# Splitting the shared value weights into the place of memT, in a two-layer decoder trunk

## The chip, the cores and the metric

The kernel runs on one core of a Trainium2 chip. The metric is the device time of one execution in microseconds (us); lower is better. Times of several runs are given as their median. The profile is of one execution, which has a time of its own; its span runs from the first instruction to the last.

## The reference

The input is one sequence of 256 positions of width 2048, a memory of 256 tokens of the same width, and fp32 weights. There are two layers. Each multiplies the residual stream by one input matrix whose columns are a main-branch input (1536), its gate (1536), memory queries (512) and their gate (512).

```python
for i in range(DEPTH):
    if i == N_A_LAYERS:
        k_blocks, v_blocks, k_mean = moba_shared_kv(h, w_kv_shared)
    u = h @ w_in[i]
    branch_in, gate_b, mem_q, gate_m = jnp.split(u, split_at, axis=-1)
    if i < N_A_LAYERS:
        branch = multiscale_pool(branch_in, pool_w[i], pool_scale[i])
    else:
        branch = moba_attention(branch_in, k_blocks, v_blocks, k_mean)
    mem_o = memory_attention(mem_q, mem, w_mem_kv[i])
    mixed = jnp.concatenate([branch * silu(gate_b), mem_o * silu(gate_m)], axis=-1)
    h = layer_norm(DEEPNORM_ALPHA * h + mixed @ w_out[i], ln_g[i], ln_b[i])
```

In the first layer the main branch is a pooling over trailing windows. In the second it is causal attention with 12 heads of 128. Its keys and values come from the shared weights `w_kv_shared`: the "shared keys" are the first 1536 columns, the "shared values" the last 1536. With 256 positions there is one attention block, so the block selection chooses nothing. In both layers there is also a 4-head attention into the memory, with keys and values `mem @ w_mem_kv[i]`.

## The kernel before

**Precision.** Every fp32 operand of TensorE is split into a high part (a copy into the type fp32r, by ScalarE, line 70) and a low part (value minus high part, by VectorE, line 71). A product is then three products: high by high, high by low and low by high.

**Items.** All weights come in blocks of 128 x 1024 fp32, 512 KB. Each block is an item in one long list, written out in the order in which TensorE uses the blocks. `run` walks the list: at step i it splits item i+3, issues the load of item i+4 on SP's queue, emits the matmuls of item i, and then whatever small steps were put down for that point (`later`). The order on each engine is therefore the order in which the program writes the instructions; no scheduler moves them. Loads land in a rotating set of four buffers `raw`; high and low parts stand in rotating sets of four buffers `wh` and `wl` each. A buffer is written again when its last readers are done. An item may name another destination: kind "act" for activations, and kind "keep" with a pair of places for the two parts; `prep_piece` then writes there and draws no `wh` and `wl`.

**Two forms of product.** `proj_t` (line 155) has the weight block stationary and the transposed activations moving: per 128 x 128 of weights one matmul of 512 columns (high weights by [high | low] activations) and one of 256 (low weights by high activations). `proj_n` (line 181) has the activations stationary and the weights moving: per block 12 matmuls of 512 columns, in triples high by high, high by low, low by high. Each accumulates in PSUM tiles `acc`.

**Tiles.** One large tile `xm` holds the transposed stream `xT` in its first half and the transposed memory `memT` in its second, each 16 blocks of 512 columns, both as views that begin SHIFT = 40 elements later than the half. At the end of the kernel the same two halves hold `kept`, views without the shift: the high and low parts of the last quarter of the second output projection, which are split ahead into it. `zT` holds the gated branches for the output projections.

```python
xm = sb.tile([P, 2 * KT * 2 * T + 128], F32R, name="xm")
KX = KT * 2 * T
xT, memT = (xm[:, SHIFT + i * KX:SHIFT + (i + 1) * KX].rearrange("p (k t) -> p k t", k=KT) for i in range(2))
kept = [xm[:, i * KX:(i + 1) * KX].rearrange("p (k n) -> p k n", k=KT) for i in range(2)]
```

**Order of the work.** First layer: memory keys and values, memory queries and gate, the pooling branch, output projection (`out_0`). Then memory keys and values of the second layer (`mem_k(1)`, `mem_v(1)`), during which the stream is normalised and transposed into `xT`; these are the last readers of `memT`. Then memory queries and gate, and three groups of four heads. A group is 8 blocks of shared keys, 8 of queries, 8 of gate (all `proj_t`), and 8 of shared values (`proj_n`, stationary `xT`). The attention steps of a group are woven in between. Last comes `out_1`, the second output projection: three quarters by items, with the kept blocks of the fourth quarter between them, then the fourth quarter from `kept` (`last`, line 715), in a closing part with the final normalisation.

Of the kernel before, what the change touches and what calls it, by code (L numbers as in the profile page):

```python
# [32 lines left out]
BLK = 1024  # L33
# [11 lines left out]
def trunk(ctx: ExitStack, tc: tile.TileContext, a: dict, out: bass.AP):  # L45
# [10 lines left out]
    xT, memT = (xm[:, SHIFT + i * KX:SHIFT + (i + 1) * KX].rearrange("p (k t) -> p k t", k=KT) for i in range(2))  # L56
# [8 lines left out]
    def mm(o, l, r, start, stop):  # L65
        nc.tensor.matmul(o, l, r, start=start, stop=stop)  # L66

    def split(hi, lo, src):

        nc.scalar.activation(hi, src, AF.Copy)  # L70
        nc.vector.tensor_sub(lo, src, f(hi))  # L71
# [12 lines left out]
    def item(src, cols, consume=None, dst=None):  # L84
        items.append(dict(src=src, cols=cols, consume=consume, dst=dst, cuts=(0, cols)))
# [69 lines left out]
    def proj_t(mov, wblk, done):  # L155


        acc = []

        def consume(kb):  # L160
            def go(wh, wl, k0=0, k1=4):
                if not acc:
                    acc.extend(ps.tile([P, 512], F32, name="acc", bufs=4) for _ in range(2))
                h = wh.rearrange("p (k n) -> p k n", n=256)
                l = wl.rearrange("p (k n) -> p k n", n=256)
                for n in range(2):
                    s = slice(n * P, (n + 1) * P)
                    for kk in range(k0, k1):
                        k = 4 * kb + kk
                        if k < KT - 1:  # L170
                            mm(acc[n], h[:, kk, s], mov[:, k], k == 0, False)
                        mm(acc[n][:, :T], l[:, kk, s], mov[:, k, :T], False, False)
                        if k == KT - 1:
                            mm(acc[n], h[:, kk, s], mov[:, k], False, True)
                    if kb == 3:
                        done(n, acc[n])
            return go
        for kb in range(4):
            item(wblk[kb], BLK, consume(kb))

    def proj_n(sta, wblk, done, korder=range(8), banks=("acc", "acc")):

        acc = []
        korder = list(korder)

        def consume(j, kb):
            def go(wh, wl):
                if j == 0:
                    acc.extend(ps.tile([P, 512], F32, name=b, bufs=4 if b == "acc" else 1) for b in banks)
                h = wh.rearrange("p (k n) -> p k n", n=512)  # L190
                l = wl.rearrange("p (k n) -> p k n", n=512)
                for t in range(2):
                    for kk in range(2):
                        k = 2 * kb + kk
                        xh = sta[:, k, t * P:(t + 1) * P]
                        xl = sta[:, k, T + t * P:T + (t + 1) * P]
                        first, last = j == 0 and kk == 0, j == 7 and kk == 1
                        mm(acc[t], xh, h[:, kk], first, False)
                        mm(acc[t], xh, l[:, kk], False, False)
                        mm(acc[t], xl, h[:, kk], False, last)  # L200
                    if j == 7:
                        done(t, acc[t])
            return go
        for j, kb in enumerate(korder):
            item(wblk[kb], BLK, consume(j, kb))

    def fold(dst, acc):
        nc.scalar.activation(dst, acc[:, T:], AF.Copy)  # L208
# [2 lines left out]
    def to_heads(dst, base):  # L211
        def done(n, acc):
            s = sb.tile([P, T], F32, name="fold", bufs=3)
            hi, lo = dst()[:, base + n, :T], dst()[:, base + n, T:]
            fold(s, acc)
            nc.vector.tensor_copy(hi, s)
            nc.vector.tensor_sub(lo, s, f(hi))
        return done

    def to_gate(dst, base):  # L220

        def done(n, acc):
            s = sb.tile([P, T], F32, name="fold", bufs=3)
            fold(s, acc)
            g = dst()

            def finish():
                th = sb.tile([P, T], F32, name="th", bufs=2)
                nc.scalar.activation(th, s, AF.Tanh, scale=0.5)
                nc.vector.scalar_tensor_tensor(g[:, base + n, :], th, 1.0, s,  # L230
                                               op0=ALU.add, op1=ALU.mult)
            later(1, finish)
        return done

    def to_values(dst):
        def done(t, acc):
            split(dst()[:, t, 0], dst()[:, t, 1], acc)
        return done

    def heads_tile(name):  # L240
        return sb.tile([P, 4, 2 * T], F32R, name=name)
# [126 lines left out]
    def plan(pr, a, b, c):  # L368

        later(a, pr.a)  # L370
        later(a + 1, pr.exps)
        later(a + 2, pr.divide)
        later(b, lambda: pr.b(0))
        later(b + 1, lambda: pr.b(1))
        later(c, pr.c)
# [68 lines left out]
    def fresh(key, make):  # L444

        tiles = []

        def g():
            if not tiles:
                tiles.append(make())  # L450
                st[key] = tiles[0]
            return tiles[0]
        return g
# [12 lines left out]
    def mem_v(layer, banks=("acc", "acc")):  # L466
        v = fresh("v", val_tile)
        proj_n(memT, [a["w_mv"][layer, kb] for kb in range(8)], to_values(v), banks=banks)

    def w_in(layer, c):  # L470
        return [a["w_in"][layer, c, kb] for kb in range(4)]

    def after(fn):

        it = items[-1]
        old = it["consume"]

        def go(*w):
            if old is not None:
                old(*w)  # L480
            fn()
        it["consume"] = go

    def mem_q_gate(layer):
        q = fresh("q", lambda: heads_tile("qq"))
        g = fresh("g", gate_tile)
        for c in range(2):
            proj_t(xT, w_in(layer, 12 + c), to_heads(q, 2 * c))
        prs = [MemPair(0, st), MemPair(2, st)]

        def go():
            plan(prs[0], 1, 5, 9)
            plan(prs[1], 7, 11, 14)
        after(go)
        for c in range(2):
            proj_t(xT, w_in(layer, 14 + c), to_gate(g, 2 * c))
# [94 lines left out]
    def out_0(n):  # L591
        proj_n(zT, [a["w_out"][0, n, kb] for kb in range(8)], to_residual(n), KORDER)
# [42 lines left out]
    mem_v(1)  # L635


    mem_q_gate(1)
    for grp in range(3):
        k = fresh("k", lambda: heads_tile("kk"))  # L640
        q = fresh("q", lambda: heads_tile("qq"))
        g = fresh("g", gate_tile)
        v = fresh("v", val_tile)
        for c in range(2):
            proj_t(xT, [a["w_sk"][2 * grp + c, kb] for kb in range(4)], to_heads(k, 2 * c))
        for c in range(2):
            proj_t(xT, w_in(1, 2 * grp + c), to_heads(q, 2 * c))
        prs = [MobaPair(2 * j, 4 * grp + 2 * j, st) for j in range(2)]

        def go(prs=prs):  # L650
            plan(prs[0], 1, 5, 17)
            plan(prs[1], 7, 18, 20)
        after(go)
        for c in range(2):
            proj_t(xT, w_in(1, 6 + 2 * grp + c), to_gate(g, 2 * c))
        proj_n(xT, [a["w_sv"][grp, kb] for kb in range(8)], to_values(v))


    def out_1():
# [25 lines left out]
    for j, it in enumerate(collect(out_1)):  # L685
# [3 lines left out]
        if j >= 8 and j % 2:  # L689
            kb = (j - 8) // 2  # L690
# [155 lines left out]
```

## Time and profile before

| | |
|---|---|
| median of 3 runs | 825.08 us (825.01 to 825.12) |
| profiled execution: its time | 824.92 us |
| its span, first to last instruction | 823.0 us |
| TensorE matmul busy | 810.0 us, 98% of the span |
| VectorE busy | 558.7 us, 68% |
| ScalarE busy | 397.1 us, 48% |
| granted TensorE clock, mean | 0.996 |

PE is TensorE's matmuls, PEld its weight loads, DVE is VectorE, ACT is ScalarE, POOL is GpSimd and SP the engine that issues most loads. L66 is line 66, the helper through which every matmul goes, so its rows are told apart by their tiles: `acc<-wh,xm` is a matmul into `acc` that reads `wh` and `xm`. A matmul's shown length reaches to its modelled end, after the next one has begun; how fast matmuls follow each other is read from their starts, or from a stretch's length over their count. An idle time in square brackets is what the engine sat idle before the instruction, with what ended it.

### The profile page before, as it was taken

The numbers are of one execution on the slowest core, as the hardware profiler recorded it, in microseconds if no ns is written. First come the engines' busy times: TensorE is split into PE (matmuls) and PEld (weight loads), VectorE is DVE, ScalarE is ACT, GpSimd is POOL, SyncE is SP. The second block draws the span as 40 slices with busy tenths as digits, with TensorE's granted clock in tenths as the row PEclk, the third lists the DMA queues.
The fourth block names the chain that finished last, engine by engine and source line by source line (L and its number), as shares of the span: only waits on it lengthen the run. The fifth ranks groups of instructions, "written<-read, shape, count | busy, mean of one in ns | idle before, by whom it ended". The sixth has DMA issues, their size and how long they took to land.

```text
span 823.0 us, 11533 instructions
## 1 busy us (share of the span) xinstructions
PE 810.0 (98%) x4436; PEld 700.7 (85%) x4436; DVE 558.7 (68%) x793; ACT 397.1 (48%) x578; POOL 0.2 (0%) x4
## 2 busy tenths in 40 slices
PE   7999999999999999999999999999999999999996
PEld 6888888898888888888888888888888888888885
DVE  5786668657956555797667667575765667568746
ACT  6564545545545343544455445344554445545520
POOL 0000000000000000000000000000000000000000
PEclk9999999999999999999999999999999999999998
DMA  8975445456557655675554544645454554646842
GB/s 311 302 251 204 173 154 191 171 181 216 179 192 283 212 191 193 203 235 201 181 179 144 189 160 173 201 156 192 169 172 169 186 188 156 185 151 224 285 130 102
DMA packets 47163, 159.13 MB, mean 193 GB/s; under 512 B 5375, under 2 KB 7167, under 8 KB 46847
## 3 DMA queue, kind: packets, MB, share of 16 engines
q1 hardware_dynamic: 46080, 155.47, 55.8%
q10 hardware_dynamic: 1028, 2.93, 0.9%
q8 instruction: 34, 0.56, 0.3%
q14 instruction: 21, 0.17, 0.1%
HBM read 156.28 MB, written 2.10 MB: 192 GB/s over the span
## 4 chain that ended last, share of the span: by engine, by line
PE 98%; DVE 1%; DMA 1%; SPq 0%; ACT 0%; issue 0%; DVEq 0%
PE acc L66 89%; PE o L66 4%; PE s L66 2%; PE pt L66 2%; DMA raw<-in_w_mk 1%; PE pt L350 0%; PE pt L300 0%; SPq L97 0%; DVE res L789 0%; PE pt L625 0%; PE o L625 0%; DVE res L770 0%; DVE wl L71 0%; ACT wh L70 0%; DVE stats L728 0%
## 5 line engine op out<-in xcount | busy, mean ns | idle before, releaser
L66 PE MATMUL acc<-xm,wh 128*128 128x512 f32 x1344 | 468.0, 395 | 4.8 <-ACT wh L70 4.5
L71 DVE TENSOR_TENSOR wl<-raw,wh 128x1024 fp32r<-128x1024 f32 (+3 forms) x274 | 324.6, 1190 | 176.8 <-ACT wh L70 174.7
L70 ACT ACTIVATE wh<-raw 128x1024 fp32r<-128x1024 f32 (+3 forms) x274 | 281.2, 1031 | 216.7 <-PE acc L66 158.6
L66 PE MATMUL acc<-xm,wl 128*128 128x256 f32 x1344 | 363.1, 280 | 0.1
L66 PEld LDWEIGHTS acc<-xm,wh 128*128 128x128 f32 x1344 | 247.9, 188 | 53.2 <-ACT wh L70 5.1
L66 PEld LDWEIGHTS acc<-xm,wl 128*128 128x128 f32 x1344 | 253.2, 188 | 7.8 <-DVE wl L71 0.8
L66 PE MATMUL acc<-wh,zT 128*128 128x512 f32 x448 | 139.9, 390 | 0.0
L66 PEld LDWEIGHTS acc<-wh,zT 128*128 128x128 f32 x448 | 84.1, 188 | 17.3
L66 PE MATMUL acc<-wl,zT 128*128 128x512 f32 x224 | 87.2, 389 | 0.0
L66 PE MATMUL acc<-wh,xm 128*128 128x512 f32 x256 | 82.6, 398 | 0.0
L66 PEld LDWEIGHTS acc<-wh,xm 128*128 128x128 f32 x256 | 48.1, 188 | 11.4
L208 ACT ACTIVATE fold<-acc 128x256 f32<-128x256 f32 x72 | 27.7, 384 | 56.8 <-PE acc L66 55.6
L66 PE MATMUL acc<-wl,xm 128*128 128x512 f32 x128 | 50.2, 392 | 0.0
L66 PEld LDWEIGHTS acc<-wl,zT 128*128 128x128 f32 x224 | 42.1, 188 | 8.5
L209 DVE TENSOR_TENSOR fold<-acc,fold 128x256 f32<-128x256 f32 x72 | 29.5, 419 | 4.8 <-ACT fold L208 4.8
L70 ACT ACTIVATE zT<-zf 128x256 fp32r<-128x256 f32 x32 | 12.9, 415 | 39.6 <-DVE zf L270 35.4
L66 PEld LDWEIGHTS acc<-wl,xm 128*128 128x128 f32 x128 | 24.1, 188 | 5.4
L71 DVE TENSOR_TENSOR xm<-raw,xm 128x1024 fp32r<-128x1024 f32 (+2 forms) x17 | 18.6, 1094 | 8.3 <-ACT xm L70 8.3
L66 PE MATMUL acc<-xm,zT 128*128 128x256 f32 (+1 forms) x144 | 22.6, 318 | 0.0
L66 PEld LDWEIGHTS acc<-xm,zT 128*128 128x128 f32 x144 | 20.7, 190 | 1.9
L70 ACT ACTIVATE ph<-pt 128x384 fp32r<-128x384 f32 (+1 forms) x20 | 10.7, 534 | 22.2 <-PE pt L350 13.5
L70 ACT ACTIVATE xm<-raw 128x1024 fp32r<-128x1024 f32 (+2 forms) x17 | 16.3, 957 | 8.0 <-DMA raw<-in_w_out 4.2
(119 smaller groups left out, 481.1 us busy)
## 6 DMA issues: line engine op xcount, KB each, us to landing
raw<-in_w_in SPq DMA_DIRECT2D x128, 512.0 KB, 3.3
raw<-in_w_out SPq DMA_DIRECT2D x64, 512.0 KB, 4.3
raw<-in_w_sk SPq DMA_DIRECT2D x24, 512.0 KB, 4.0
raw<-in_w_sv SPq DMA_DIRECT2D x24, 512.0 KB, 3.2
raw<-in_w_mv SPq DMA_DIRECT2D x14, 512.0 KB, 5.3
raw<-in_w_mk SPq DMA_DIRECT2D x12, 512.0 KB, 4.3
raw<-in_xT SPq DMA_DIRECT2D x4, 512.0 KB, 4.8
res<-in_x ACTq DMA_DIRECT2D x2, 1024.0 KB, 5.4
```

Source lines behind the costliest of these rows:

```text
L66: nc.tensor.matmul(o, l, r, start=start, stop=stop)
L70: nc.scalar.activation(hi, src, AF.Copy)
L71: nc.vector.tensor_sub(lo, src, f(hi))
L208: nc.scalar.activation(dst, acc[:, T:], AF.Copy)
L209: nc.vector.tensor_add(dst, acc[:, :T], dst)
```

## The change

`proj_n` gets an argument `place`. Where it is given, item j goes to the two places that `place(j)` names, by kind "keep". The shared values of the three groups name a quarter of `memT`: four of its 16 blocks of 512 columns, the first two for the high part of a weight block, the other two for the low part, and the quarters in turns of four. So 24 blocks are split into `memT` and not into `wh` and `wl`, and the moving operand of their matmuls is read from `xm`, as the stationary one is. All other items are as they were.

```diff
-    def proj_n(sta, wblk, done, korder=range(8), banks=("acc", "acc")):
+    def proj_n(sta, wblk, done, korder=range(8), banks=("acc", "acc"), place=None):
...
         for j, kb in enumerate(korder):
-            item(wblk[kb], BLK, consume(j, kb))
+            item(wblk[kb], BLK, consume(j, kb), dst=place and ("keep", *place(j)))
...
     mem_v(1)
 
 
+    def in_mem(j):
+
+        return [memT[:, 4 * (j % 4) + 2 * i:4 * (j % 4) + 2 * i + 2].rearrange("p k n -> p (k n)") for i in range(2)]
+
     mem_q_gate(1)
     for grp in range(3):
...
-        proj_n(xT, [a["w_sv"][grp, kb] for kb in range(8)], to_values(v))
+        proj_n(xT, [a["w_sv"][grp, kb] for kb in range(8)], to_values(v), place=in_mem)
```

## The prediction

> **What bounds the kernel now.** I read the page's busy times first, then its chain of work that ended last, then TensorE's waits, and last the stretches of the shared values in time.
>
> ```profile
> span 823.0 us, 11533 instructions
> PE 810.0 (98%) x4436; PEld 700.7 (85%) x4436; DVE 558.7 (68%) x793; ACT 397.1 (48%) x578; POOL 0.2 (0%) x4
> ...
> PE 98%; DVE 1%; DMA 1%; SPq 0%; ACT 0%; issue 0%; DVEq 0%
> ...
> PE acc L66 <- ACT wh L70: 4.5, 1, 4.5
> PE pt L777 <- DVE cc L774: 2.8, 1, 2.8
> PE acc L66 <- ACT cct L779: 0.4, 1, 0.4
> PE acc L66 <- DVE xm L71: 0.3, 1, 0.3
> ```
>
> The last four rows are all the waits of TensorE's matmuls (total, times, longest). Each happened once, at the start (first blocks, 4.5 and 0.3) or in the closing part (lines 777 and 779). Between them TensorE never waited for a weight block. So 98% of the chain is matmul, and an edit in the middle moves the time only if it makes TensorE wait, or if it changes how fast the matmuls follow each other.
>
> The windows below (stretch, its length, then busy time and count of PE, PEld, DVE, ACT, POOL, then clock, DMA share, GB/s) show the rate. The first is first-layer output projection after the last pooling product, the next three are the shared values of the three groups, the last is second-layer output projection.
>
> ```profile
> 260.81:336.99 76.18, 76.18 (x338) 63.07 (x337) 44.46 (x46) 32.15 (x33) 0.00 (x0) 1.00 0.59 200
> 507.25:529.64 22.39, 22.39 (x97) 18.02 (x96) 13.08 (x19) 11.61 (x20) 0.00 (x0) 1.00 0.57 188
> 603.23:625.62 22.39, 22.39 (x97) 18.02 (x96) 13.08 (x19) 11.61 (x20) 0.00 (x0) 1.00 0.56 188
> 699.21:721.60 22.39, 22.39 (x97) 18.02 (x96) 13.07 (x19) 11.60 (x20) 0.00 (x0) 1.00 0.63 187
> 735.98:790.44 54.46, 54.46 (x242) 45.11 (x242) 41.95 (x47) 30.41 (x32) 0.00 (x0) 1.00 0.73 244
> ```
>
> All are proj_n: 12 matmuls of 128x512 per block, in the same order (high stationary by high weights, by low weights, low stationary by high weights), clock 1.00. The windows touch a neighbour, so I count by blocks: 28 blocks, 336 matmuls in 76.18 us are 226.7 ns each; 8 blocks, 96 matmuls in 22.39 us are 233.2 ns each; 20 blocks, 240 matmuls in 54.46 us are 226.9 ns. The shared values run 6.5 ns per matmul slower than output projections of the same form, with nothing waited for. The DMA share does not explain it: it is highest, 0.73, where the matmuls are fast.
>
> **The change, part by part.** Twenty-four blocks (8 in each of three groups) get their high part and low part in memT's half of the tile xm instead of the rotating wh and wl. Nothing is added or taken away in loads, splits or matmuls, and the order on each engine is the same.
>
> Splits (lines 70 and 71), 24 of each: only the place of the output changes. The trace has the same split into xm, for the blocks that are kept at the end:
>
> ```profile
> L70 ACT ACTIVATE wh<-raw 128x1024 fp32r<-128x1024 f32 x258 | 271.5, 1057 | 207.8 <-PE acc L66 155.2 <-issue 15.3 <-DMA raw<-in_w_out 13.6
> L70 ACT ACTIVATE xm<-raw 128x1024 fp32r<-128x1024 f32 x14 | 14.8, 1058 | 6.7 <-DMA raw<-in_w_out 4.2 <-DMA raw<-in_memT 1.3 <-DMA raw<-in_xT 1.0
> L71 DVE TENSOR_TENSOR wl<-raw,wh 128x1024 fp32r<-128x1024 f32 x258 | 314.1, 1223 | 170.8 <-ACT wh L70 168.7 <-PE acc L66 1.4
> L71 DVE TENSOR_TENSOR xm<-raw,xm 128x1024 fp32r<-128x1024 f32 x14 | 17.1, 1219 | 4.3 <-ACT xm L70 4.3
> ```
>
> ScalarE 1058 against 1057 ns, VectorE 1219 against 1223: no cost, on engines that are busy 11.6 and 13.1 of 22.39 us.
>
> Waits for a free place: within a group four places in turns hold as many blocks as four buffers of wh, so blocks 5 to 8 wait for blocks 1 to 4 as before. Blocks 1 to 4 find a place last read long ago, and the first three blocks behind the eight find wh and wl free. These waits of ScalarE go (start, length, engine, line, what, idle before and its releaser):
>
> ```profile
> 515.89 1.06 ACT L70 ACTIVATE wh<-raw 128x1024 fp32r<-128x1024 f32 x1 [1.74 <-PE acc L66]
> 521.45 1.06 ACT L70 ACTIVATE wh<-raw 128x1024 fp32r<-128x1024 f32 x1 [1.74 <-PE acc L66]
> 524.25 1.06 ACT L70 ACTIVATE wh<-raw 128x1024 fp32r<-128x1024 f32 x1 [1.74 <-PE acc L66]
> 527.04 1.06 ACT L70 ACTIVATE wh<-raw 128x1024 fp32r<-128x1024 f32 x1 [1.74 <-PE acc L66]
> 516.99 1.23 DVE L71 TENSOR_TENSOR wl<-raw,wh 128x1024 fp32r<-128x1024 f32 x1 [1.13 <-ACT wh L70]
> ```
>
> The first row is the split of block 7 of the first group, which stays in step with TensorE; its low part is done at 516.99 + 1.23 = 518.22, and TensorE comes to it at 507.25 + 6 x 2.80 = 524.05. That lead of 5.8 us is the cover: the 1.74 us waits in the next three rows (the following group's first blocks) were never on the path, so taking them away is worth nothing. Had the cover been gone, each would cost 1.74 us, nine in all. Behind them ScalarE next meets the split of the finished values, which waits for TensorE, so it cannot run further ahead.
>
> Loads: the 24 DMAs on SP's queue keep their order and size. A raw buffer comes free a little earlier, so some loads behind the eight blocks start up to some 5 us earlier (an estimate: the split at 527.04 could follow the one of block 8 and two more, at about 522), into a queue that TensorE does not wait for. No cost; POOL has none.
>
> ```profile
> raw<-in_w_sv SPq DMA_DIRECT2D x24, 512.0 KB, 3.2
> 743.23 1.05 ACT L70 ACTIVATE xm<-raw 128x1024 fp32r<-128x1024 f32 x1
> ```
>
> The last row is the first kept block written over the same half of xm. It comes at 743.23, after the values' last matmul at 721.60, so the new readers hold nothing up. In the built program TensorE has one more wait in each group, on a matmul of its own 104 instructions back: long done, nothing.
>
> What is left is the rate of the 288 matmuls (24 blocks by 12). Here the place matters by its offset. xT and memT are views of xm shifted by SHIFT = 40 elements, 160 bytes; kept (line 57), zT, wh and wl are not shifted, and in the built program all these tiles begin alike modulo 512 bytes. So far the values' stationary operand (xT) is shifted and the moving one (wh, wl) is not; afterwards both are. That pair stands nowhere in the trace, but the other three do (start, length to the modelled end, count):
>
> ```profile
> 290.53 0.61 PE L66 MATMUL acc<-wh,zT 128*128 128x512 f32 x2
> 291.21 0.61 PE L66 MATMUL acc<-wh,zT 128*128 128x512 f32 x2
> ...
> 510.28 0.39 PE L66 MATMUL acc<-wl,xm 128*128 128x512 f32 x1
> 510.98 0.39 PE L66 MATMUL acc<-wl,xm 128*128 128x512 f32 x1
> ...
> 486.07 0.39 PE L66 MATMUL acc<-xm,wh 128*128 128x512 f32 x1
> 486.30 0.28 PE L66 MATMUL acc<-xm,wl 128*128 128x256 f32 x1
> 487.81 0.39 PE L66 MATMUL acc<-xm,wh 128*128 128x512 f32 x1
> ...
> 791.81 2.65 PE L66 MATMUL acc<-xm,zT 128*128 128x512 f32 x11
> 801.80 4.36 PE L66 MATMUL acc<-xm,zT 128*128 128x256 f32 x35
> ...
> L66 PEld LDWEIGHTS acc<-wh,zT 128*128 128x128 f32 x448 | 84.1, 188 | 17.3
> L66 PEld LDWEIGHTS acc<-wh,xm 128*128 128x128 f32 x256 | 48.1, 188 | 11.4
> ```
>
> Neither shifted: a triple takes 291.21 - 290.53 = 0.68 us. Stationary shifted: 510.98 - 510.28 = 0.70 us. Moving shifted (proj_t): five pairs of a 512 and a 256 take 487.81 - 486.07 = 1.74 us, 348 ns a pair; unshifted matmuls of these sizes, from the kept rows, take (2.65 - 0.39) / 10 = 226 and (4.36 - 0.28) / 34 = 120 ns (0.39 and 0.28 being the modelled lengths of one), 346 to 347 together. So a shift of the moving operand alone costs about 1 ns in two matmuls, and one of the stationary operand alone 6.5 ns in one, though its weight load lasts 188 ns in both rows and ends inside the matmul before it.
>
> Bounds of the unknown pair: from the equal offsets, 226.7 ns, 288 x -6.5 = -1.87 us; to the shifts adding up and the moving one now costing what the stationary one does, 239.7 ns, +1.87 us. I take the lower end. What the slow rows have and the fast ones lack is two reads at unequal offsets with the stationary one ahead; a load that is no longer by itself, and a moving shift that is nearly free, speak for how the two meet and not for either shift alone. Equal offsets then meet as the unshifted pairs do.
>
> The Trainium skill speaks against it: "SBUF — State Buffer", section "Who interferes with whom", has TensorE read through two independent ports, one for the moving operand and one for the weight load, and has it wait for no one. By that rule the place of an operand would not change the rate and the sum would be zero; this case's trace does not agree, with 226.7 and 233.2 ns for one form at one clock.
>
> **Sum.** 0 (splits) + 0 (waits) + 0 (loads) - 1.87 us (rate). The profiled execution took 824.92 us, 823.0 of it span, and would come to 823.05. The median of the runs is 825.08, 0.16 above it: 823.2 us.
>
> **The rivals.** First, no change (825.1 us). The shifted stationary operand costs its 6.5 ns wherever the moving one lies, so 0.70 us a triple stays; the waits that go were hidden. For it: every row of a shifted stationary operand is slow, and none shows a cure. Against it: the equal 188 ns loads. A cure of less than 5.7 ns per matmul (0.2% of 825.08 is 1.65 us, over 288) lands here too.
>
> Second, slower: the two shifts add. The place is the same 288 matmuls; both operands now begin inside a unit in which the unshifted ones begin at its start, the price is again up to 6.5 ns each, 825.08 + 1.87 = 826.95 us, say 827.0, and it decides from 5.7 ns up. For it: the 512-wide matmuls of proj_t, moving operand shifted, begin 486.30 - 486.07 = 0.23 us before the next, 230 ns or so against 226.7. Against it: their 256-wide partners make that good, 348 against 347.
>
> A third, that the splits come late because their places are now read by TensorE longer, needs the 5.8 us lead gone; four places in turns keep it, so I give it no chance of its own.
>
> **How the numbers follow.** Equal offsets, faster: 0.48, 823.2. No change: 0.33, 825.1. Slower: 0.19, 827.0. What a measurement of this kernel can tell from no change I set at 0.2%, 1.65 us. The range takes in the first two cases and the near half of the third: from 822.8 (0.4 below the forecast, a rate of 225.3 ns) to 826.0. The likeliest case's own range is 822.8 to 823.6.
>
> **What would show it.** Right: the three stretches last 8 x 12 x 226.7 ns = 21.77 instead of 22.39 us, triples at 0.68 us, all later times shifted by 0.6, 1.2 and 1.9 us, ScalarE's 1.74 us waits behind the eight blocks gone, and TensorE's four waits unchanged. Wrong: triples of 0.70 us or more, or a fifth wait of TensorE in these stretches.

## The result, and the profile after

The changed kernel takes **823.56 us** (median; 823.07 to 826.31), the kernel before, measured beside it, 825.78 us (824.31 to 826.51). The ratio is 0.9981, with a 95% interval of 0.9973 to 0.9988: faster, by 1 to 2 us. Measured a second time, beside the kernel before, it was 0.9978 (0.9969 to 0.9988). The forecast was 823.2 us against 825.08, a ratio of 0.9977.

The page of the changed kernel, whose profiled execution took 824.99 us:

```profile
span 822.4 us, 11515 instructions
PE 809.3 (98%) x4436; PEld 701.7 (85%) x4436; DVE 558.5 (68%) x793; ACT 396.7 (48%) x578; POOL 0.2 (0%) x4
...
PE 93%; DVE 3%; DMA 2%; issue 1%; ACT 1%; SPq 0%; DVEq 0%; ACTq 0%
```

The span is only 0.6 us shorter than before, less than the medians say, and the chain has steps of other engines that the chain before did not have. So the stretches have to be looked at one by one. Here are the shared values of the three groups, and then the stretch of the second output projection that the prediction showed for the kernel before (stretch, its length, busy time and count of PE, PEld, DVE, ACT, POOL, then clock, DMA share, GB/s):

```profile
507.57:529.35 21.78, 21.78 (x98) 18.02 (x96) 13.16 (x19) 11.51 (x20) 0.00 (x0) 1.00 0.66 217
602.93:624.71 21.78, 21.78 (x97) 18.03 (x96) 13.16 (x19) 11.51 (x20) 0.00 (x0) 1.00 0.66 218
698.30:720.08 21.78, 21.78 (x97) 18.03 (x96) 13.16 (x19) 11.52 (x20) 0.00 (x0) 1.00 0.65 218
734.46:789.72 55.26, 54.77 (x242) 45.04 (x242) 41.93 (x47) 30.30 (x32) 0.00 (x0) 1.00 0.70 237
```

Each group of shared values lasts 21.78 us instead of 22.39: 226.9 ns per matmul (21.78 / 96), the rate of the output projections. Three times 0.61 is 1.83 us, and it is there in the starts of what follows. The stretch of the output projection starts at 734.46 instead of 735.98, which is 1.52 us earlier (the first group itself began 0.32 us later, at 507.57 against 507.25: the start of the kernel took that much longer in this execution). Then 0.8 us is given back inside the output projection: 55.26 against 54.46 us. TensorE's waits, and its matmuls at that place, show how:

```profile
PE acc L66 <- ACT wh L70: 4.3, 1, 4.3
PE pt L781 <- DVE cc L778: 2.8, 1, 2.8
PE acc L66 <- DVE wl L71: 0.5, 1, 0.5
PE acc L66 <- ACT cct L783: 0.4, 1, 0.4
```

```profile
772.38 0.61 PE L66 MATMUL acc<-wh,zT 128*128 128x512 f32 x2
773.49 0.50 PE L66 MATMUL acc<-wl,zT 128*128 128x512 f32 x1 [0.49 <-DVE wl L71]
773.82 0.63 PE L66 MATMUL acc<-wh,zT 128*128 128x512 f32 x2
```

The third wait is new. At 773 us a low part of one block of the output projection came late; from 772.38 to 773.49 TensorE needs 1.11 us for two matmuls that take 0.45 us elsewhere. This also explains the chain: it runs back through that late block to a split and a load, and what lies before it is no longer matmul alone. Nothing of the sort happens in the shared values. Whether the change causes the late block is asked below.

ScalarE around the end of the first group (start, length, engine, line, what, idle before it and what ended it):

```profile
515.99 1.06 ACT L70 ACTIVATE xm<-raw 128x1024 fp32r<-128x1024 f32 x1 [1.66 <-PE acc L66]
518.66 1.06 ACT L70 ACTIVATE xm<-raw 128x1024 fp32r<-128x1024 f32 x1 [1.61 <-PE acc L66]
519.63 2.21 ACT L70 ACTIVATE wh<-raw 128x1024 fp32r<-128x1024 f32 x2
...
528.18 0.60 ACT L70 ACTIVATE vv<-acc 128x512 fp32r<-128x512 f32 x1 [4.61 <-PE acc L66]
```

The waits of 1.74 us ahead of the three blocks that follow are gone, and most of the idle time (4.61 us) has moved to the split of the finished values, which waits for TensorE in any case.

### The profile page after: what moved, and what is told of

It is laid out like the page before. It is cut to its first block, busy times and chain, and to the rows that moved or that the text cites. A ratio compares the mean times of both kernels' runs of the same rounds, so it can differ in the third digit from the quotient of the medians.

```text
span 822.4 us, 11515 instructions
## 1 busy us (share of the span) xinstructions
PE 809.3 (98%) x4436; PEld 701.7 (85%) x4436; DVE 558.5 (68%) x793; ACT 396.7 (48%) x578; POOL 0.2 (0%) x4
## 4 chain that ended last, share of the span: by engine, by line
PE 93%; DVE 3%; DMA 2%; issue 1%; ACT 1%; SPq 0%; DVEq 0%; ACTq 0%
PE acc L66 84%; PE o L66 4%; PE s L66 2%; PE pt L66 2%; DMA raw<-in_w_out 1%; DVE wl L71 1%; DMA raw<-in_w_mk 1%; PE pt L350 0%; ACT wh L70 0%; PE pt L300 0%; DVE xm L71 0%; SPq L97 0%; DVE res L383 0%; DVE stats L384 0%; DVE res L793 0%
## 5 line engine op out<-in xcount | busy, mean ns | idle before, releaser
L71 DVE TENSOR_TENSOR wl<-raw,wh 128x1024 fp32r<-128x1024 f32 (+2 forms) x250 | 295.2, 1187 | 149.4 <-ACT wh L70 148.2
L70 ACT ACTIVATE wh<-raw 128x1024 fp32r<-128x1024 f32 (+2 forms) x250 | 255.9, 1028 | 187.3 <-PE acc L66 133.6
L66 PE MATMUL acc<-xm 128*128 128x512 f32 x288 | 65.8, 390 | 0.0
L66 PEld LDWEIGHTS acc<-xm 128*128 128x128 f32 x288 | 54.1, 188 | 11.1
L71 DVE TENSOR_TENSOR xm<-raw,xm 128x1024 fp32r<-128x1024 f32 (+2 forms) x41 | 47.8, 1171 | 22.1 <-ACT xm L70 21.9
L70 ACT ACTIVATE xm<-raw 128x1024 fp32r<-128x1024 f32 (+2 forms) x41 | 41.3, 1015 | 19.0 <-PE acc L66 9.8
L66 PE MATMUL acc<-wh,xm 128*128 128x512 f32 x64 | 21.6, 404 | 0.0
L71 DVE TENSOR_TENSOR zT<-zf,zT 128x256 fp32r<-128x256 f32 x32 | 12.9, 423 | 9.7 <-ACT zT L70 9.7
```

## The experiments

Two explanations could give the shorter stretches. By the prediction's theory the addresses do it: both operands of a matmul now begin 160 bytes past a multiple of 512. By the main rival theory it is something else that came with the change: ScalarE's removed waits, the four additional buffers, or both operands lying in one tile. The first three runs separate these; the later ones ask which offsets count and for which form, what the lead is worth, and where the late block comes from.

### The same places, 512 bytes past the half

```diff
     def in_mem(j):
-        return [memT[:, 4 * (j % 4) + 2 * i:4 * (j % 4) + 2 * i + 2].rearrange("p k n -> p (k n)") for i in range(2)]
+        c0 = KX + 128 + 2048 * (j % 4)
+        return [xm[:, c0 + i * BLK:c0 + (i + 1) * BLK] for i in range(2)]
```

> The changed kernel, with its four places moved on in xm so that they begin 512 bytes past the half and not 160: same number of places, same waits, same tile, but the moving operand again at the offset that wh and wl have modulo 512 bytes, with the stationary xT still shifted by 160. If the gain comes from how the two offsets meet, the 96 matmuls of a group go back to 233.2 ns each (22.39 us a group) and the time to that of the kernel before, 825.1 us or ratio 1.000. If the gain comes from the freed buffers and waits, or from reading both operands out of one tile, the matmuls stay at 226.9 ns (21.78 us) and the ratio at 0.998.

It took 825.42 us against 825.41 before: ratio 1.0, interval 0.999 to 1.0009. One of its three stretches of shared values, which agree within 0.01 us:

```profile
508.77:531.17 22.40, 22.40 (x97) 18.02 (x96) 13.20 (x19) 11.40 (x20) 0.00 (x0) 1.00 0.62 212
```

And ScalarE behind the first group:

```profile
521.14 2.00 ACT L70 ACTIVATE wh<-raw 128x1024 fp32r<-128x1024 f32 x2
...
529.97 0.60 ACT L70 ACTIVATE vv<-acc 128x512 fp32r<-128x512 f32 x1 [5.12 <-PE acc L66]
```

All that came with the change is there (the same tile, four buffers more, no wait ahead of the next group's blocks) and only the offset is that of `wh` and `wl` again. The whole gain is gone. So the buffers and the removed waits are worth nothing, and the offset is worth everything. This is the plainest run of the study.

### The kernel before, with no shift at all

```diff
-SHIFT = 40
+SHIFT = 0
```

> The kernel before with SHIFT = 0: nothing of the change, all operands at the same offset modulo 512 bytes. If equal offsets are what counts, the shared values run at 226.7 ns without any change of place, and so do the memory values (12 blocks of 16 not disturbed by transposes); 40 blocks x 12 x 6.5 ns = 3.1 us less from these. For proj_t, whose moving operand is the shifted one, the trace of before has no equal pair; put together from other rows a 512 and a 256 would take 347 ns against 347.5, nothing, so 822.0 us in all. If instead the shift is what keeps proj_t fast, its 1344 pairs get slower and the time ends above 825. If the freed buffers made the gain, the shared values stay at 233.2 ns.

It took 828.63 us: ratio 1.0036 (1.0023 to 1.0048), slower than before. Two stretches, a long run of `proj_t` blocks and the shared values of the first group:

```profile
457.40:488.49 31.09, 31.09 (x178) 26.96 (x177) 20.94 (x33) 14.25 (x19) 0.00 (x0) 1.00 0.55 184
511.47:533.25 21.78, 21.78 (x98) 18.03 (x97) 13.02 (x19) 11.62 (x20) 0.00 (x0) 1.00 0.60 192
```

The same `proj_t` blocks in the kernel before:

```profile
453.77:484.35 30.58, 30.58 (x179) 26.87 (x178) 20.85 (x33) 14.26 (x19) 0.00 (x0) 1.00 0.55 187
```

The shared values are as fast as after the change, with `wh`, `wl` and the waits of the kernel before: equal offsets are enough, and it need not be 160 bytes. But `proj_t` is slower. Eleven blocks, 88 pairs of a 512 and a 256, take 31.09 us instead of 30.58: 353.3 against 347.5 ns a pair, 5.8 ns more. There are 1344 such pairs in the kernel; all of them at this price would lose 7.8 us. Added up from the starts of the matmuls in both traces, they lose 6.0 us (without the first 16 pairs, which fall into the start of the kernel), while the shared values gain 1.9 us and the memory values 0.8 us. So not all pairs pay the whole price. Two stretches of 32 pairs in this kernel show it, the first behind score matmuls of the shared attention, the second behind score matmuls of the memory attention:

```profile
489.87:501.04 11.17, 11.17 (x67) 9.75 (x66) 8.63 (x15) 5.59 (x13) 0.00 (x0) 1.00 0.51 172
414.67:425.98 11.31, 11.31 (x66) 9.81 (x65) 7.89 (x13) 6.85 (x14) 0.00 (x0) 1.00 0.48 149
```

The kernel before takes 11.12 and 11.13 us for the same pairs. In the first stretch the offset hardly shows, in the second it shows in full. Which pairs escape, and why, is not settled here. So the shift helps `proj_t` and hurts the shared values.

### The weight buffers shifted as well

```diff
+    pad = sb.tile([P, SHIFT], F32, name="pad")
+    nc.gpsimd.memset(pad, 0.0)
```

The pad stands ahead of `raw`, `wh` and `wl` in the kernel before, so these begin 160 bytes later, as `xT` and `memT` do. Only `zT` is left without a shift.

> The kernel before with a pad of 160 bytes ahead of raw, wh and wl: weights, xT and memT are all shifted, zT alone is not. Relation of the offsets: the shared values at 226.7 ns as with no shift at all, proj_t at whatever the kernel without a shift shows, and the output projections (moving shifted by 160, stationary not) at a rate that the trace of before has not shown for this form: 226.7 if a shifted moving operand is free, up to 233.2 if it costs what a shifted stationary one does. If a shifted stationary operand costs its 6.5 ns by itself, the shared values stay at 233.2.

One execution took 832.77 us, beside 825.41 before. The first output projection, the `proj_t` stretch and the shared values:

```profile
263.51:342.22 78.71, 78.71 (x338) 63.29 (x337) 44.54 (x46) 32.16 (x33) 0.00 (x0) 1.00 0.61 197
459.61:490.70 31.09, 31.09 (x179) 26.98 (x178) 20.95 (x33) 14.25 (x19) 0.00 (x0) 1.00 0.55 184
513.67:535.45 21.78, 21.78 (x98) 18.03 (x97) 13.02 (x19) 11.62 (x20) 0.00 (x0) 1.00 0.59 193
```

Three readings. The shared values are fast with both operands shifted, in the rotating buffers. `proj_t` has equal offsets again and is slow to the hundredth as with no shift. And the output projection, whose moving operand alone is now shifted, slows from 76.18 to 78.71 us: 234.3 ns per matmul (78.71 / 336) against 226.7. So in `proj_n` it makes little difference which of the two operands is shifted (234.3 ns here, 233.2 for the shared values before). What counts is that one is shifted against the other.

### Twelve distances

```diff
     def in_mem(j):
-        return [memT[:, 4 * (j % 4) + 2 * i:4 * (j % 4) + 2 * i + 2].rearrange("p k n -> p (k n)") for i in range(2)]
+        d = SHIFT + 8 * (4 * st["grp"] + j % 4)
+        c0 = KX + d + 2048 * (j % 4)
+        return [xm[:, c0 + i * BLK:c0 + (i + 1) * BLK] for i in range(2)]
```

The moving operand lies 0, 32, 64, ... 352 bytes further than the stationary one, four distances in each group.

> The changed kernel, with the places of the 24 blocks at twelve distances from xT's offset, 0 to 352 bytes in steps of 32 (two blocks each; first group 0, 32, 64, 96, second 128 to 224, third 256 to 352). If the relation of the offsets counts, the triples take 0.68 us at distance 0 and 0.70 at 352, which is the distance that wh had from xT modulo 512, with one or more edges between. If any place in memT is fast, all 24 blocks take 2.72 us. If only a place of equal offset is fast, 22 of 24 take 2.80.

It took 826.25 us in one execution, beside 825.41. The first four blocks of each group, one row each (12 matmuls; only TensorE's columns: stretch, length, busy and count, clock, DMA share, GB/s):

```profile
508.04:510.78 2.74, 2.74 (x13) 1.00 0.36 88
510.78:513.59 2.81, 2.81 (x14) 1.00 0.29 111
513.59:516.34 2.75, 2.75 (x13) 1.00 0.54 186
516.34:519.16 2.82, 2.82 (x14) 1.00 0.87 260
603.88:606.65 2.77, 2.77 (x13) 1.00 0.35 109
606.65:609.46 2.81, 2.81 (x14) 1.00 0.30 90
609.46:612.25 2.79, 2.79 (x14) 1.00 0.50 179
612.25:615.04 2.79, 2.79 (x14) 1.00 0.90 250
699.82:702.56 2.74, 2.74 (x13) 1.00 0.36 93
702.56:705.37 2.81, 2.81 (x14) 1.00 0.27 104
705.37:708.12 2.75, 2.75 (x13) 1.00 0.61 192
708.12:710.94 2.82, 2.82 (x14) 1.00 0.84 221
```

The last four rows (256 to 352 bytes) repeat the first four (0 to 96) to the hundredth of a microsecond, while the middle four (128 to 224) differ: the spacing goes by the distance **modulo 256 bytes**. Distance 0 is fastest (2.74 us; the first block of a group starts with a slower triple), 64 is next (2.75), and 32, 96 and 160 are slowest (2.81 to 2.82). A block's first matmuls still go at a rate of the block before: in the second turn of a group, where distance 0 follows 96, it takes 2.76 us, no less than 64. That 0 is fastest rests on the changed kernel too, where each block behind the first takes 2.72 us. The spacing by the distance modulo 256 also fits the two slow cases above: before the change the values' moving operand lay 160 bytes behind, which is 96 modulo 256 (22.39 / 8 = 2.80 us a block), and in the run with shifted weight buffers 160 ahead (78.71 / 28 = 2.81). The DMA share runs from 0.27 to 0.90 through these rows and has nothing to do with it.

The rule that the prediction quoted from the Trainium skill ("SBUF — State Buffer", "Who interferes with whom": two independent read ports of TensorE) would give twelve equal rows. These rows do not agree with it as a statement on speed.

### Shared-key blocks at twelve distances

```diff
             proj_t(xT, [a["w_sk"][2 * grp + c, kb] for kb in range(4)], to_heads(k, 2 * c))
+            for kb, it in enumerate(items[-4:]):
+                c0 = KX + SHIFT + 8 * (4 * grp + kb) + 2048 * kb
+                it["dst"] = ("keep", xm[:, c0:c0 + BLK], xm[:, c0 + BLK:c0 + 2 * BLK])
```

The changed kernel, with the blocks of the shared keys (`proj_t`, weights stationary) in `memT` too, to find a distance that suits `proj_t` better than the one it has.

> The changed kernel, with the 24 blocks of the shared keys (proj_t: weights stationary, xT moving) also split into memT, at twelve distances from xT's offset, 0 to 352 bytes in steps of 32 (group 0: 0, 32, 64, 96; then 128 to 224; then 256 to 352; each twice). The kernels without a shift and with shifted weights showed proj_t at equal offsets slower than at 160 bytes, some 353 against 348 ns a pair. If the distance alone sets it, the blocks at 0 and 256 take 8 x 353 = 2.83 us, the one at 96 (moving ahead by 160 modulo 256, as now) 2.78 us, and it repeats every 256 bytes as the shared values did. If the pair depends on the absolute place instead, all blocks take alike.

No distance did better. Where no other form stands between them, blocks of eight pairs took 2.79 to 2.82 us, against 2.77 to 2.79 in the kernel before; distance 96, at which the two operands lie to each other modulo 256 bytes as they do in the kernel before, was among the best, with 2.79. But this run took **848.73 us**, 23 us more than before, for a reason that was not meant. The keys of a group are split into the places that the values of the group before were just being read from, so their splits wait for TensorE. TensorE's wait, then one stall and the stretch behind it with its clock, and last the stretch behind the sixth stall:

```profile
PE acc L66 <- DVE xm L71: 14.4, 6, 2.4
```

```profile
521.60:524.01 2.41, 0.00 (x1) 0.00 (x1) 1.23 (x1) 1.06 (x1) 0.00 (x0) 1.00 0.74 231
524.01:528.60 4.59, 4.59 (x12) 3.31 (x12) 0.00 (x0) 0.00 (x0) 0.00 (x0) 0.63 0.44 137
645.88:648.75 2.87, 2.87 (x12) 2.36 (x13) 0.54 (x1) 0.60 (x1) 0.00 (x0) 1.00 0.55 181
```

The prediction's third way, splits that come late because their places are still read, is what this run shows by accident, with its price. The stall lasts 2.41 us, from the last read of a place through ScalarE (1.06) and VectorE (1.23) to TensorE, and behind it 12 matmuls take 4.59 us instead of 2.72, at a granted clock of 0.63. One such stall costs about 2.4 + 1.9 = 4.3 us (worked out from these rows). Six at that price are 26 us, and the run lost 23: behind the second and third the clock fell as low, behind the fourth and fifth to 0.67 and 0.68, and behind the sixth, which was as long, not at all (2.87 us for 12 matmuls). The Trainium skill's "TensorE: Matmul & The Clock Gate", Part 1, has the clock fall after an idle window of about 3.4 us; here 2.4 us of idle time was enough five times out of six.

### The kept blocks spread out

```diff
+    KEPT_AT = (5, 7, 10, 12, 15, 17, 20, 22)
...
-        if j >= 8 and j % 2:
-            kb = (j - 8) // 2
+        if j in KEPT_AT:
+            kb = KEPT_AT.index(j)
```

The changed kernel again. The kept blocks of the second output projection are two extra splits between the items; from item 9 on they come behind every second item. If this crowding makes the late block at 773 us, an earlier and looser order should take it away.

> The changed kernel, with the eight kept blocks among the items of the second output projection from item 5 on, two in every five items, in place of every second item from 9 on. Same work. In the profile of the changed kernel TensorE waited 0.65 us for a low part at 772.6 us, in the stretch in which kept blocks double the loads; the profiles of the other kernels show 0 to 0.65 us at that place. If these loads are what is late, the wait is gone here and the median falls by what it costs on average, 0.2 to 0.5 us, below the changed kernel run beside it. If the wait was a chance of that one execution, no difference.

It took 825.57 us against 825.49 before (ratio 1.0001, 0.9992 to 1.001): the gain of the change is lost, though the shared values still take 21.78 us a group. TensorE's waits in the output projection, and the two places:

```profile
PE acc L66 <- DVE wl L71: 1.6, 2, 0.8
```

```profile
750.37 0.61 PE L66 MATMUL acc<-wh,zT 128*128 128x512 f32 x2
751.77 0.50 PE L66 MATMUL acc<-wl,zT 128*128 128x512 f32 x1 [0.79 <-DVE wl L71]
...
773.22 0.61 PE L66 MATMUL acc<-wh,zT 128*128 128x512 f32 x2
774.60 0.50 PE L66 MATMUL acc<-wl,zT 128*128 128x512 f32 x1 [0.77 <-DVE wl L71]
```

Now two blocks are late, by 0.95 and 0.93 us (1.40 and 1.38 us for two matmuls of 0.45), 1.9 us together, as much as the change had gained. The order that was meant to relieve the place made it worse. It put the eight kept blocks among 18 items instead of 15, so it spread them only a little, and crowding by their loads is neither shown nor ruled out. What it shows is that this stretch, with a DMA share of 0.7, has so little lead that up to 1.9 us come and go.

### The change again

The changed kernel itself, beside the run before.

> The changed kernel itself once more, beside the two above. Shared values 21.78 us a group again; 1.9 us under the kernel before, ratio 0.998. If the late low part in the second output projection is part of the change, it shows again near 772 us; if it is chance, it differs.

It took 823.8 us (823.07 to 824.91) against 825.49; ratio 0.9978 (0.9969 to 0.9988). The first group's values and all of TensorE's waits:

```profile
507.42:529.20 21.78, 21.78 (x97) 18.02 (x96) 13.24 (x19) 11.51 (x20) 0.00 (x0) 1.00 0.68 217
```

```profile
PE acc L66 <- DVE xm L71: 4.6, 2, 4.4
PE pt L781 <- DVE cc L778: 2.8, 1, 2.8
PE acc L66 <- ACT cct L783: 0.4, 1, 0.4
```

Here there is no late block, and the last quarter of the output projection starts at 788.78 against 790.45 us before. That is 1.67 us earlier, which is 1.84 less the 0.17 us by which the first group began later (507.42 against 507.25). With the same kernel the late block is there in one execution and not in another. It is in none of the profiles of the kernel before, of the one without a shift, and of the one with a shift of 96 bytes, and in that with the spread kept blocks twice; most of the others have a shorter or longer one there, at the same matmul each time, and one of them, with the weight buffers shifted, is without the change (0.3 us). Whether the change makes it likelier would need many profiles of each and stays open.

### The memory values too

```diff
-    zT = sb.tile([P, KT, 2 * T], F32R, name="zT")
+    zm = sb.tile([P, KT * 2 * T + 128], F32R, name="zT")
+    zT = zm[:, :KT * 2 * T].rearrange("p (k t) -> p k t", k=KT)
...
-        proj_n(memT, [a["w_mv"][layer, kb] for kb in range(8)], to_values(v), banks=banks)
+        proj_n(memT, [a["w_mv"][layer, kb] for kb in range(8)], to_values(v), banks=banks,
+               place=lambda j: [zm[:, SHIFT + (2 * (j % 4) + i) * BLK:SHIFT + (2 * (j % 4) + i + 1) * BLK] for i in range(2)])
```

The changed kernel, with the 16 blocks of the memory values of both layers put at equal offsets as well, in four places of `zT`, which is not in use then.

> The changed kernel, with the weight blocks of the memory values of both layers (16 blocks, stationary memT, shifted) also at equal offset: split into four places of zT, which is 128 columns longer for it, shifted by 160 bytes like memT. Relation of the offsets: these 192 matmuls go from 233.2 to 226.7 ns too, 1.25 us less than the changed kernel, so 3.1 us less than the kernel before, ratio 0.9962. If it were the tile xm or the place of memT and not the offset, nothing more than the changed kernel's 0.998.

It took 823.63 us (821.93 to 823.95) against 825.94 before: ratio 0.9969, interval 0.9959 to 0.998. The first two blocks of the first layer's memory values:

```profile
12.80:18.29 5.49, 5.49 (x27) 4.51 (x26) 4.87 (x5) 3.60 (x4) 0.00 (x0) 1.00 1.03 419
```

In the kernel before:

```profile
12.36:17.95 5.59, 5.59 (x26) 4.51 (x25) 4.36 (x5) 4.25 (x4) 0.00 (x0) 1.00 1.03 418
```

0.10 us in 24 matmuls is 4 ns each, less than the 6.5 of the shared values. In the second layer, where transposes stand between the blocks, it is 2 to 4 ns. Added up from the starts of all 192 matmuls it is 0.76 us, where 1.25 was expected. The ratio is the best of the study, but its interval overlaps that of the change (0.9969 to 0.9988), so it is not shown to beat it.

### A shift of 96 bytes

```diff
-SHIFT = 40
+SHIFT = 24
```

The changed kernel with another absolute place and still equal offsets in the shared values.

> The changed kernel with SHIFT = 24, 96 bytes in place of 160. The shared values keep equal offsets, at another absolute place: 21.78 us a group if the relation counts, something else if the place does. proj_t gets a distance of moving minus stationary of 96 bytes, where the twelve offsets of the key blocks gave 2.806 us a block (stationary ahead by 160) against 2.78 to 2.79 now: 168 blocks x 0.02 us, 2.7 to 4.4 us more in all, so 826.5 to 828.5.

It took 827.63 us in one execution, beside 825.94. The `proj_t` stretch and the first group's values:

```profile
456.99:487.86 30.87, 30.87 (x179) 26.91 (x177) 20.89 (x33) 14.24 (x19) 0.00 (x0) 1.00 0.57 185
510.93:532.72 21.79, 21.79 (x97) 18.02 (x96) 13.15 (x19) 11.39 (x20) 0.00 (x0) 1.00 0.65 218
```

The shared values stay fast, at 0, 96 and 160 bytes alike: the absolute place does not count. `proj_t` at a distance of 96 bytes takes 350.8 ns a pair (30.87 / 88), between 347.5 at 160 and 353.3 at 0.

## Why the prediction was right, and where it was not

**The rate of the 288 matmuls (the whole sum).** Right in mechanism and size: 22.39 became 21.78 us where 21.77 was forecast, in sum 1.83 against 1.87 us. The medians fell by 2.2 and 1.7 us in two measurements. That the relation of the two reads does it, not either shift by itself, was argued from what three rows had and lacked. The first experiment shows it for the change, and the run with shifted weight buffers and the twelve distances show it from the other side.

**The rivals.** No change needed the stationary operand's shift to cost by itself: it does not, as the changed kernel's own stretches show with `xT` still shifted. Slower needed the two shifts to add: they cancel. The late splits were given no chance, since four places in turns keep the lead. That held; the run with the key blocks shows the price where they do not.

**Splits, waits, loads at nothing.** Right, and shown by the run with the same places and an offset of 512 bytes: ratio 1.0 with all of these and without the rate. ScalarE's idle time went on to the split of the finished values, as described.

**"A moving shift that is nearly free."** This step was wrong, though the conclusion drawn with its help held. In `proj_n` a moving shift alone costs 7.6 ns per matmul (234.3 against 226.7), about as much as a stationary one (6.5). In `proj_t` it gains 5.8 ns a pair in the long stretch. The 348 ns for a shifted moving operand were read rightly, the long stretch has 347.5; but the 346 to 347 set beside it was put together from kept matmuls of another order, not from this form without a shift, which takes 353.3 there. So one of the two reasons for taking the lower bound was false, and with the true price of a moving shift in `proj_n` the rival of two shifts that add up would have looked stronger: that it came out at the lower bound was in part luck. The general form of the argument does not hold either, since in `proj_t` equal offsets are the slow case. Had I drawn the further conclusion that the shift could as well go, the run without it shows the bill: 3.2 us slower (828.63 against 825.41), not faster.

**TensorE's four waits unchanged.** Not quite. The profiled execution has a late block in the second output projection, outside the stretches in question, for 0.8 us with what surrounds it. Together with a start that took 0.3 us longer it hides 1 of the 1.8 us in that one span. The second profile of the same kernel does not have it; how many of the timed executions do is not known.

## What to carry to other kernels

When matmuls of one form run at two rates at the same clock with nothing waited for, compare where the two operands begin within 256 bytes before looking at waits or buffers, and then try the distance for each form by itself, since the best one for one form may be the worst for another. Read a form's rate from a long undisturbed stretch of that very form, from the start of its first matmul to the start of what follows, and not from numbers put together from its neighbours. A gain of a quarter of a per cent can be given back by one late block elsewhere, so settle it by stretches in the trace and by medians, not by one span.

## What the runs showed of the hardware

The spacing of these matmuls goes by the distance of moving and stationary operand modulo 256 bytes, in steps that are not monotonic: in `proj_n` 0 is fastest (226.7 ns), 64 nearly so (2.75 us a block), 32, 96 and 160 slowest (2.80 to 2.82). In `proj_t`, equal offsets, the best case of `proj_n`, are the worst of the three distances that were tried over the whole kernel: 353.3 ns a pair at 0, 350.8 at 96, 347.5 at 160. Why a distance is fast, the traces don't show. Neither do they show why a stream behind another form runs at a rate of its own for some matmuls.

Five of six stalls of 2.4 us were followed by 12 matmuls at a granted clock of 0.61 to 0.68, the sixth by 12 at 1.00. So a stall of this length can cost nearly twice what the wait itself shows; what decides whether it does, the traces don't show.
